# Turning probabilities, convolution and merged branch with VectorE and DRAM instead of TensorE, in a hybrid decoder layer

## The chip, the cores and the metric

The kernel runs on one core of one Trainium2 chip. The metric is the device time of one execution in microseconds (us). A core has TensorE (matrix products, PE in the profile; PEld is its weight load), VectorE (DVE), ScalarE (ACT), GpSimd (POOL) and SyncE (SP), which run side by side, each through its own queue in order, and wait for each other through semaphores.

## The reference

One sub-layer of a decoder on 256 tokens and 2048 features, in float32. Two token mixers run in parallel, each with a SiLU gate path, then a merge by sigmoid gates and an output projection:

```python
h = _rmsnorm(x, pre_norm_g)
proj = h @ w_in
(q_a, c_kv, k_rope, z_mla, c_in, b_gate, c_gate, z_conv, g_mla, g_conv) = split(proj)

q = _rmsnorm(q_a, q_a_norm_g) @ w_q_b        # 16 heads, 128 + 64 (rotary)
kv = _rmsnorm(c_kv, kv_a_norm_g) @ w_kv_b    # 16 heads, 128 + 128
attn = causal_softmax(q k^T / sqrt(192)) v   # 256 x 2048
y_mla = (attn * silu(z_mla)) @ w_o_mla

u = c_gate * c_in
conv = conv_w[0] * u[s-2] + conv_w[1] * u[s-1] + conv_w[2] * u[s]
y_conv = (b_gate * conv * silu(z_conv)) @ w_o_conv

merged = sigmoid(g_mla) * y_mla + sigmoid(g_conv) * y_conv
x = x + _rmsnorm(merged @ w_out, post_norm_g)
```

## The kernel before

Every float32 operand of a product is split into a high and a low part (`split_act`, lines 227 to 234: ScalarE writes the high part, VectorE subtracts it to get the low one), and a product is three matmuls: high x high, high x low, low x high. All matmuls are recorded at line 88, all turns on TensorE at line 91.

The weights come from DRAM in units of 1 MB (`raw`, three buffers, issued by SyncE at line 148). A unit is split in two halves `whi` and `wlo` of 128x1024 (five buffers each). `take(i)` hands out unit i and, before that, writes out the loads up to unit i+2 and the split of unit i+1. The order of units is the list `order`, which follows the order of the work.

A schedule by a timeline model orders each engine's instructions; what is wrapped in `tc.keep_in_program_order` is pinned behind everything written before it on its engine. TensorE's matmuls and turns, and the DMAs that GpSimd issues, are all pinned.

Stage 1, the head loop (16 heads, 29 to 44 us each in the chain): for head h, `z` (the gate, one unit), `scores(h)` (`sc`), and the four units of `channels(h, 0..3)` (`cv`), which compute one 512-wide column block of one of the four convolution inputs, h % 4 naming which one and h // 4 naming the block j. Beside them stand the head groups: `a` (the matmuls `qn` and `kn` of the next two heads), `r` (`qr`), and every fourth head `v` (`vv`). `scores` leaves the probabilities `p` (128 queries x 384: block one sees 128 keys, block two 256; last written at line 589). `turn(h, p)` turns its three 128x128 blocks on TensorE into a PSUM bank `tp` and splits that into `pt`; `values(h, ...)` multiplies with v (`o`) and writes `at_f`.

The convolution needs `u` shifted by one and two tokens: `taps(j, t)` (t is the half of 128 tokens) moves shifted copies `mv` and the tap weights `cw` with DMAs on GpSimd's queue (line 664) in steps that the loop calls with `next(tap)`. When the gates are there, `channels_join(j, t)` multiplies them in, in place, in `cv_f` (seen by rows of tokens as `cv_t`).

Stage 2, four column groups c, each four sweeps of four units (`tokens(c, n, cols)`, matmuls `sq`): the two gates from `x_both`, then `at_both` x w_o_mla, then `cv_both` x w_o_conv. `split_branch` splits `at_f` into `at_both` in the first sweep of group 0; `turn_branch` turns the eight convolution blocks on TensorE (bank `ct`, four turns each) in its second and third sweep. The memory of `at_both` and `cv_both` is the one that the head loop's temporaries held. The merged blocks `m` (two per group, in the tile `sg`) are turned on TensorE by `features` (bank `mt`) into `m_both`, after the next group's first sweep.

Stage 3: `out`, four column groups of four units from `m_both`; the last merged group is turned after the first unit of the first group. The end is the norm and the store.

Of the kernel before, what the change touches and what calls it, by code (L numbers as in the profile page):

```python
# [11 lines left out]
F32 = mybir.dt.float32  # L12
# [6 lines left out]
P = 128  # L19
# [63 lines left out]
def tile_layer(ctx: ExitStack, tc: tile.TileContext, xw, x, pos, pvec, post_g, wc, wz, wcv, wkr, wqk, wqr, wv, cwr, wsq, out):  # L83
# [6 lines left out]
    def transpose(*a):  # L90
        return tc.keep_in_program_order(nc.tensor.transpose(*a))  # L91
# [7 lines left out]
    top.tile([P, 184], F32, name="top_pad")  # L99
    wpool = ctx.enter_context(tc.tile_pool(name="wpool", bufs=1))  # L100
    psum = ctx.enter_context(tc.tile_pool(name="psum", bufs=1, space=PSUM))


    plan = []
# [104 lines left out]
    def bank(name, tag="mm", bufs=4):  # L209
        return psum.tile([P, 512], F32, name=name, tag=tag, bufs=bufs)  # L210
# [16 lines left out]
    def split_act(hi, lo, src, keep=False):  # L227
        a = nc.scalar.activation(hi, src, AF.Copy)  # L228
        b = nc.vector.tensor_tensor(lo, src, hi.bitcast(F32), op=ALU.subtract)  # L229
        if keep:  # L230

            tc.keep_in_program_order(a)
            tc.keep_in_program_order(b)
# [57 lines left out]
    def temp(name, shape=(P, S), dt=F32, bufs=2, tag=None):  # L291

        tag, n = tag or name.rstrip("0123456789_"), shape[-1]
        if n % LINE == 0:
            return bp.tile(list(shape), dt, name=name, tag=tag, bufs=bufs)
        return bp.tile([P, -(-n // LINE) * LINE], dt, name=name, tag=tag, bufs=bufs)[:, :n]


    def split_scaled(dst, src, k):
# [251 lines left out]
    def scores(h):  # L551

        (qn, kn), qr = groups["a", h // HG], groups["r", h // HG]
        j = h % HG
        sc = bank(f"sc{h}", tag="st", bufs=1)
        t0, t1 = slice(0, P), slice(P, S)
        mm = matmul
        o = sc[:, :S].rearrange("p (i k) -> p i k", i=2)
        mm(o, qn[0][:, j, t0], kn[:, :, j, :P], start=True, stop=False)
        mm(sc[:, :P], qn[1][:, j, t0], kn[:, 0, j, :P], start=False, stop=False)  # L560
        mm(o, qr[:, j, t0], kr[:, :, :P], start=False, stop=True)
        o = sc[:, S:]
        product(o, [a[:, j, t1] for a in qn], [kn[:, i, j, :] for i in range(2)], True, False)
        for i in range(2):
            mm(o, qr[:, j, t1], kr[:, i, :], start=False, stop=i == 1)
        if h == 0:
            temp("pad", (P, 4 * LINE), bufs=1)
        p = temp("p", (P, 3 * P), bufs=1)
        half = temp("sc_half", (P, P), bufs=1)
        nc.scalar.activation(half[:, :], sc[:, P:S], AF.Copy)  # L570
        nc.vector.tensor_tensor(p[:, :P], sc[:, :P], half[:, :], op=ALU.add)
        nc.vector.tensor_tensor(p[:, :P], p[:, :P], mask[:, :P], op=ALU.add)
        nc.vector.tensor_tensor(p[:, P:], sc[:, S:], mask[:, P:], op=ALU.add)
        mx, sm, rs = temp("mx", (P, NT)), temp("sm", (P, NT)), temp("rs", (P, NT))
        nb = temp("nb", (P, NT))
        for t in range(NT):
            o = slice(t * P, (2 * t + 1) * P)
            nc.vector.reduce_max(mx[:, t : t + 1], p[:, o], axis=mybir.AxisListType.X)
        nc.vector.tensor_scalar(nb[:, :], mx[:, :], -SCALE, None, op0=ALU.mult)
        for t in range(NT):  # L580
            o = slice(t * P, (2 * t + 1) * P)
            nc.scalar.activation(
                p[:, o], p[:, o], AF.Exp, bias=nb[:, t : t + 1], scale=SCALE,
                accum_out=sm[:, t : t + 1],
            )
        nc.vector.reciprocal(rs[:, :], sm[:, :])
        for t in range(NT):
            o = slice(t * P, (2 * t + 1) * P)
            nc.vector.tensor_scalar(p[:, o], p[:, o], rs[:, t : t + 1], None, op0=ALU.mult)
        return p  # L590

    def turn(h, p):

        tp = bank(f"tp{h}", tag="st", bufs=1)
        for b in range(3):
            transpose(tp[:, b * P : (b + 1) * P], p[:, b * P : (b + 1) * P], ident[:, :])
        pt = temp("pt", (P, 2, 3 * P), F32R, 1)
        split_act(pt[:, 0, :], pt[:, 1, :], tp[:, : 3 * P])
        return pt

    def values(h, pt, sz):
# [52 lines left out]
    def channels_join(j, t):  # L654
        u, w = cv_t[:, j, t, :], cv_w[:, t, :]
        nc.vector.tensor_tensor(u, u, w, op=ALU.mult)

    def taps(j, t):

# [35 lines left out]
    for h in range(H):  # L695

        tapped = h % 4 == 2 or (h > 0 and h % 4 == 0) or h == H - 1
        sz_new = silu("sz", project(u_head[h][0], f"z{h}"))
        if h == 0:
            latent_turn("qa", qa, "q_g", (("st", 1), ("o", 1)))  # L700

            def turn_keys():
                latent_turn("ckv", ckv, "kv_g", (("mm", 4), ("mm", 4)))
                next(table_parts)

            channels(h, 0, turn_keys)
            for i in first:
                make(*i)
            key_rope()
            channels(h, 1)  # L710
            channels(h, 2)
            p = scores(h)
        elif h == 1:

            pt = turn(0, p)
            channels(h, 0)
            values(0, pt, sz)
            p = scores(h)
            channels(h, 1)
            channels(h, 2)  # L720
            pt = turn(h, p)
        else:
            p = scores(h)
            channels(h, 0)
            channels(h, 1)
            pt = turn(h, p)
            if tapped:
                next(tap)
            channels(h, 2)
            values(h, pt, sz_new)  # L730
            if tapped:
                next(tap)
        for i in made[h]:
            make(*i)
        if h == 1:
            values(h, pt, sz_new)
        sz = sz_new
        channels(h, 3)
        if h % 4 == 0 and h > 0:
            for t in range(NT):  # L740
                channels_join(h // 4 - 1, t)
        if h % 4 == 1:
            tap = taps(h // 4, 1)
            next(tap)
        elif h % 4 == 3 and h + 1 < H or h == H - 2:
            tap = taps(h // 4, 0)
            next(tap)
    for t in range(NT):
        channels_join(3, t)


    bstack.close()
# [8 lines left out]
            hs = slice(h, h + 2)  # L761
            split_act(at_both[:, hs, :S], at_both[:, hs, S:], at_f[:, hs, :], True)

    def turn_branch(i):

        j, t = divmod(i, NT)
        turned(f"ct{i}", cv_t[:, j, t, :], cv_both, j, t)

    def turned(name, src, both, c, t):
        tp = bank(name, tag=("st", "o")[t], bufs=1)  # L770
        for j in range(4):
            transpose(tp[:, j * P : (j + 1) * P], src[:, j * P : (j + 1) * P], ident[:, :])
        ks, ts = slice(4 * c, 4 * c + 4), slice(t * P, (t + 1) * P)
        lo = slice(t * P + S, (t + 1) * P + S)
        split_act(both[:, ks, ts], both[:, ks, lo], tp[:, :].rearrange("p (k q) -> p k q", k=4))

    def tokens(c, n, cols):

        pss = [bank(f"sq{c}_{n}_{t}") for t in range(NT)]
        for kk in range(4):  # L780
            w = take(u_d[c][n][kk])
            if c == 0 and n == 0:
                split_branch(kk)
            if c == 0 and n in (1, 2):
                turn_branch(4 * (n - 1) + kk)
            for t in range(NT):
                for k4 in range(4):
                    k = 4 * kk + k4
                    a = [cols[:, k, o + t * P : o + (t + 1) * P] for o in (0, S)]
                    product(pss[t][:, :], a, w(k4, 512), k == 0, k == KD - 1)  # L790
        return pss
# [4 lines left out]
    def features(c, m, m_both):  # L796

        for t in range(NT):
            turned(f"mt{c}_{t}", m[t], m_both, c, t)

    waiting = m_both = None
    for c in range(4):
# [18 lines left out]
        for t in range(NT):  # L821
            nc.vector.tensor_tensor(m[t][:, :], pss[t][:, :], m[t][:, :], op=ALU.mult)
        pss = tokens(c, 3, cv_both)
        for t in range(NT):
            y = gates[1][t]
            nc.vector.tensor_tensor(y[:, :], pss[t][:, :], y[:, :], op=ALU.mult)
            nc.vector.tensor_tensor(m[t][:, :], m[t][:, :], y[:, :], op=ALU.add)
        waiting = m
    def out_product(ps, t, w, kk):
        ts = slice(t * P, (t + 1) * P)  # L830
# [6 lines left out]
            out_product(pss[t], t, w, kk)  # L837

    pss = [bank(f"out0_{t}") for t in range(NT)]
    out_products(pss, take(u_out[0][0]), 0)  # L840
    features(3, waiting, m_both)
    main.close()


# [35 lines left out]
    for c in range(3):  # L880
        if c:
            pss = [bank(f"out{c}_{t}") for t in range(NT)]
        for kk in range(0 if c else 1, 4):
            out_products(pss, take(u_out[c][kk]), kk)
        for t in range(NT):
            out_block(c, t, pss[t])
# [99 lines left out]
```

## Time and profile before

| | before |
|---|---|
| median of 3 runs | 1053.18 us (1053.15 to 1053.72) |
| profiled execution | 1052.91 us |
| its span, first to last instruction | 1050.9 us |
| TensorE busy | 1041.9 us, 99% |
| VectorE busy | 670.0 us, 64% |
| ScalarE busy | 560.3 us, 53% |
| GpSimd busy | 71.4 us, 7% |
| granted TensorE clock | 0.998 |

A row of the chain gives the start in us from the span's start, the length, and the piece of work with its count of instructions. A row of a timeline gives start, length, engine, line, operation, output <- input, and in brackets the idle time before it and what ended that. A group row (line, engine, operation, shapes, count) gives busy us and mean ns. TensorE's matmuls are pipelined, so the length of one is a latency, and a busy TensorE isn't one at its peak. In a table of windows each pair is the engine's busy us and its instruction count.

### The profile page before, as it was taken

Reading aid. Unit: us, or ns where it says so; the run is one execution under the profiler, and the core shown is the slowest. Engines: PE = TensorE matmul, PEld = TensorE weight load, DVE = VectorE, ACT = ScalarE, POOL = GpSimd, SP = SyncE. Lnnn points to the kernel's source line nnn. Section 1 sums busy time; section 2 is a strip of 40 time slices with the busy share of each in tenths; the row PEclk is TensorE's granted clock in tenths of the full one; section 3 lists DMA queues with packets and bytes.
Section 4 is the critical chain, followed back from the end, with each engine's and each line's share of the span. In section 5 each row is a group of like instructions: output and inputs, shape, how many; then the busy total and the mean of one; then the engine's idle time right before and its main releaser. Section 6 shows DMA issues by size and latency. Waiting matters only on the chain.

```text
span 1050.9 us, 12889 instructions
## 1 busy us (share of the span) xinstructions
PE 1041.9 (99%) x4934; PEld 874.3 (83%) x4934; DVE 670.0 (64%) x954; ACT 560.3 (53%) x770; POOL 71.4 (7%) x147
## 2 busy tenths in 40 slices
PE   9999999999999999999999999999999999999996
PEld 8888888888888888888888888888888888888885
DVE  7588668676686777866777764554554455445562
ACT  7776556556665566655655464444434434444450
POOL 7620011000110001100011000000000000000000
PEclk9999999999999999999999999999999999999999
DMA  8745566455665555845567555455555555558542
GB/s 332 298 173 200 201 219 207 165 210 200 210 215 196 189 192 175 273 172 193 188 203 236 202 184 196 166 195 200 190 187 184 200 200 190 176 195 314 196 171 80
DMA packets 33884, 212.13 MB, mean 202 GB/s; under 512 B 4320, under 2 KB 5024, under 8 KB 10912
## 3 DMA queue, kind: packets, MB, share of 16 engines
q1 hardware_dynamic: 29808, 197.54, 52.1%
q0 software_dynamic: 3584, 10.50, 4.2%
q10 hardware_dynamic: 432, 3.29, 0.8%
q8 instruction: 38, 0.62, 0.2%
q14 instruction: 22, 0.18, 0.0%
HBM read 205.05 MB, written 2.10 MB: 197 GB/s over the span
## 4 chain that ended last, share of the span: by engine, by line
PE 98%; issue 1%; DVE 0%; POOL 0%; ACT 0%; POOLq 0%; DVEq 0%; ACTq 0%
PE cv L88 33%; PE sq L88 33%; PE z L88 8%; PE out L88 7%; PE qn L88 2%; PE kn L88 2%; PE qa L88 2%; PE vv L88 2%; PE ckv L88 2%; PE sc L88 1%; PE qr L88 1%; PE o L88 1%; PE tp L91 0%; PE idle L88 0%; PE kr L88 0%
## 5 line engine op out<-in xcount | busy, mean ns | idle before, releaser
L229 DVE TENSOR_TENSOR wlo<-raw,whi 128x1024 fp32r<-128x1024 f32 (+1 forms) x370 | 440.3, 1199 | 309.4 <-ACT whi L228 285.5
L228 ACT ACTIVATE whi<-raw 128x1024 fp32r<-128x1024 f32 (+1 forms) x372 | 383.5, 1036 | 379.2 <-PE sq L88 186.3
L88 PE MATMUL cv<-whi,x_both 128*128 128x512 f32 x1024 | 325.4, 391 | 0.0
L88 PEld LDWEIGHTS cv<-whi,x_both 128*128 128x128 f32 x1024 | 192.3, 188 | 38.9
L88 PE MATMUL cv<-wlo,x_both 128*128 128x512 f32 x512 | 199.5, 390 | 0.0
L88 PE MATMUL sq<-whi,x_both 128*128 128x512 f32 x512 | 160.2, 391 | 0.0
L88 PEld LDWEIGHTS sq<-whi,x_both 128*128 128x128 f32 x512 | 96.1, 188 | 19.9
L88 PEld LDWEIGHTS cv<-wlo,x_both 128*128 128x128 f32 x512 | 96.2, 188 | 18.5
L88 PE MATMUL sq<-wlo,x_both 128*128 128x512 f32 x256 | 99.6, 389 | 0.0
L88 PE MATMUL sq<-whi,at_both 128*128 128x512 f32 x256 | 80.4, 391 | 0.0
L88 PE MATMUL sq<-whi,cv_both 128*128 128x512 f32 x256 | 79.5, 389 | 0.0
L88 PE MATMUL out<-whi,m_both 128*128 128x512 f32 x256 | 79.2, 390 | 0.0
L88 PE MATMUL z<-x_both,whi 128*128 128x512 f32 x256 | 60.7, 389 | 0.0
L88 PEld LDWEIGHTS sq<-whi,cv_both 128*128 128x128 f32 x256 | 48.0, 188 | 10.0
L88 PEld LDWEIGHTS sq<-whi,at_both 128*128 128x128 f32 x256 | 48.1, 188 | 9.9
L88 PEld LDWEIGHTS out<-whi,m_both 128*128 128x128 f32 x256 | 48.0, 188 | 9.9
L88 PEld LDWEIGHTS z<-x_both,whi 128*128 128x128 f32 x256 | 48.0, 188 | 9.9
L88 PEld LDWEIGHTS sq<-wlo,x_both 128*128 128x128 f32 x256 | 48.1, 188 | 9.8
L88 PE MATMUL sq<-wlo,at_both 128*128 128x512 f32 x128 | 49.8, 389 | 0.0
L88 PE MATMUL sq<-wlo,cv_both 128*128 128x512 f32 x128 | 49.8, 389 | 0.0
L88 PE MATMUL out<-wlo,m_both 128*128 128x512 f32 x128 | 49.8, 389 | 0.0
L88 PEld LDWEIGHTS z<-x_both,wlo 128*128 128x128 f32 x256 | 32.8, 191 | 1.2
(208 smaller groups left out, 1031.1 us busy)
## 6 DMA issues: line engine op xcount, KB each, us to landing
raw<-wsq_dram SPq DMA_DIRECT2D x80, 1024.0 KB, 4.7
raw<-wcv_dram SPq DMA_DIRECT2D x64, 1024.0 KB, 4.8
raw<-wz_dram SPq DMA_DIRECT2D x16, 1024.0 KB, 4.8
raw<-wqk_dram SPq DMA_DIRECT2D x8, 1024.0 KB, 6.0
cw<-cwr_dram POOLq DMA_DIRECT2D x24, 256.0 KB, 5.7
raw<-wc_dram SPq DMA_DIRECT2D x4, 1024.0 KB, 9.9
raw<-wv_dram SPq DMA_DIRECT2D x4, 1024.0 KB, 6.7
cv_f<-x_dram SPq DMA_DIRECT2D x1, 2048.0 KB, 9.5
```

Source lines behind the costliest of these rows:

```text
L88: return tc.keep_in_program_order(nc.tensor.matmul(*a, **kw))
L228: a = nc.scalar.activation(hi, src, AF.Copy)
L229: b = nc.vector.tensor_tensor(lo, src, hi.bitcast(F32), op=ALU.subtract)
```

## The change

The 112 turns on TensorE of `tp`, `ct` and `mt` are replaced. Each tile of 128 tokens by n x 128 columns (n = 3 for the probabilities, 4 for a convolution or merged block) goes this way: VectorE turns every 32x32 block into a second tile (`via`, one buffer; for the merged blocks the tile of the other gate); four DMAs, one for each quarter of 32 partitions, write it to a DRAM tile `far` in pieces of n x 32 numbers so that each row of `far` is one row of the turned tile; one DMA brings it back to the place it came from. All five stand on GpSimd's queue in program order, and the one back waits for the four. The split then reads the turned tile from chip memory, not from PSUM, through `by_rows` and `quarters`, which only reorder the view, and it is pinned.

The order changes too. The split of the probabilities comes later: in odd heads but the last before the group `a`, with `values` behind that group; in the others behind what `made` names, with `values` behind the fourth convolution unit. `channels_join` for t = 1 comes one head earlier, at h % 4 == 3, and turns its block at once. The last join's `via` is the tile `mv2`. The merged blocks are turned right where they are made, both with their DMAs out before the DMAs back, and the last group's split comes before the third unit of stage 3, not after its first. The sixteen turns of the two latents (`lt_qa`, `lt_ckv`) stay on TensorE.

```diff
@@ -99,6 +99,8 @@
     top.tile([P, 184], F32, name="top_pad")
     wpool = ctx.enter_context(tc.tile_pool(name="wpool", bufs=1))
     psum = ctx.enter_context(tc.tile_pool(name="psum", bufs=1, space=PSUM))
+    dram = ctx.enter_context(tc.tile_pool(name="dram", bufs=1, space=bass.MemoryType.DRAM))
     plan = []
@@ -294,6 +296,40 @@
         if n % LINE == 0:
             return bp.tile(list(shape), dt, name=name, tag=tag, bufs=bufs)
         return bp.tile([P, -(-n // LINE) * LINE], dt, name=name, tag=tag, bufs=bufs)[:, :n]
+    def turned(src, via, n):
+        via = via[:, : P * n]
+        v = via.rearrange("p (q k x) -> p q k x", q=4, k=n)
+        nc.vector.transpose(v.rearrange("p q k x -> p k q x"), src)
+        far = dram.tile([P, P * n], F32, name="far", tag=f"far{n}", bufs=2)
+        def go():
+            f = far[:, :].rearrange("(q y) (i m) -> i y q m", q=4, i=4)
+            for i in range(4):
+                m = via[32 * i : 32 * i + 32, :].rearrange("y (q m) -> y q m", q=4)
+                tc.keep_in_program_order(nc.gpsimd.dma_start(out=f[i], in_=m))
+        def come(dst):
+            tc.keep_in_program_order(nc.gpsimd.dma_start(out=dst, in_=far[:, :]))
+        return go, come
+    def turned_back(src, via, n):
+        go, come = turned(src, via, n)
+        go()
+        come(src)
+    def by_rows(t, n):
+        return t.rearrange("p (i k x) -> p k i x", i=4, k=n)
+    def quarters(t):
+        return t.rearrange("p k (i x) -> p k i x", i=4)
+    def via():
+        return temp("via", (P, 512), bufs=1)
     def split_scaled(dst, src, k):
@@ -587,15 +623,14 @@
         for t in range(NT):
             o = slice(t * P, (2 * t + 1) * P)
             nc.vector.tensor_scalar(p[:, o], p[:, o], rs[:, t : t + 1], None, op0=ALU.mult)
+        turned_back(p[:, :], via(), 3)
         return p
-    def turn(h, p):
-        tp = bank(f"tp{h}", tag="st", bufs=1)
-        for b in range(3):
-            transpose(tp[:, b * P : (b + 1) * P], p[:, b * P : (b + 1) * P], ident[:, :])
+    def turn(p):
         pt = temp("pt", (P, 2, 3 * P), F32R, 1)
-        split_act(pt[:, 0, :], pt[:, 1, :], tp[:, : 3 * P])
+        hi, lo = (pt[:, j : j + 1, :].rearrange("p o (k q) -> p (o k) q", k=3) for j in range(2))
+        split_act(quarters(hi), quarters(lo), by_rows(p[:, :], 3), True)
         return pt
     def values(h, pt, sz):
@@ -654,6 +689,7 @@
     def channels_join(j, t):
         u, w = cv_t[:, j, t, :], cv_w[:, t, :]
         nc.vector.tensor_tensor(u, u, w, op=ALU.mult)
+        turned_back(u, via() if t or j < 3 else temp("mv2", (P, 512), bufs=1, tag="mv2x"), 4)
     def taps(j, t):
@@ -695,6 +731,8 @@
     for h in range(H):
         tapped = h % 4 == 2 or (h > 0 and h % 4 == 0) or h == H - 1
+        early_values = h % 2 and h < H - 1
         sz_new = silu("sz", project(u_head[h][0], f"z{h}"))
         if h == 0:
             latent_turn("qa", qa, "q_g", (("st", 1), ("o", 1)))
@@ -712,41 +750,43 @@
             p = scores(h)
         elif h == 1:
-            pt = turn(0, p)
             channels(h, 0)
-            values(0, pt, sz)
+            values(0, turn(p), sz)
             p = scores(h)
             channels(h, 1)
             channels(h, 2)
-            pt = turn(h, p)
         else:
             p = scores(h)
             channels(h, 0)
             channels(h, 1)
-            pt = turn(h, p)
             if tapped:
                 next(tap)
             channels(h, 2)
-            values(h, pt, sz_new)
             if tapped:
                 next(tap)
         for i in made[h]:
+            if i[0] == "a":
+                pt = turn(p)
             make(*i)
-        if h == 1:
-            values(h, pt, sz_new)
+            if i[0] == "a":
+                values(h, pt, sz_new)
+        if h > 0 and not early_values:
+            pt = turn(p)
         sz = sz_new
         channels(h, 3)
+        if h > 0 and not early_values:
+            values(h, pt, sz_new)
         if h % 4 == 0 and h > 0:
-            for t in range(NT):
-                channels_join(h // 4 - 1, t)
+            channels_join(h // 4 - 1, 0)
+        if h % 4 == 3:
+            channels_join(h // 4, 1)
         if h % 4 == 1:
             tap = taps(h // 4, 1)
             next(tap)
         elif h % 4 == 3 and h + 1 < H or h == H - 2:
             tap = taps(h // 4, 0)
             next(tap)
-    for t in range(NT):
-        channels_join(3, t)
+    channels_join(3, 0)
     bstack.close()
@@ -761,18 +801,15 @@
             hs = slice(h, h + 2)
             split_act(at_both[:, hs, :S], at_both[:, hs, S:], at_f[:, hs, :], True)
-    def turn_branch(i):
-        j, t = divmod(i, NT)
-        turned(f"ct{i}", cv_t[:, j, t, :], cv_both, j, t)
-    def turned(name, src, both, c, t):
-        tp = bank(name, tag=("st", "o")[t], bufs=1)
-        for j in range(4):
-            transpose(tp[:, j * P : (j + 1) * P], src[:, j * P : (j + 1) * P], ident[:, :])
+    def split_turned(src, both, c, t):
         ks, ts = slice(4 * c, 4 * c + 4), slice(t * P, (t + 1) * P)
         lo = slice(t * P + S, (t + 1) * P + S)
-        split_act(both[:, ks, ts], both[:, ks, lo], tp[:, :].rearrange("p (k q) -> p k q", k=4))
+        split_act(quarters(both[:, ks, ts]), quarters(both[:, ks, lo]), by_rows(src, 4), True)
+    def split_channels(i):
+        j, t = divmod(i, NT)
+        split_turned(cv_t[:, j, t, :], cv_both, j, t)
     def tokens(c, n, cols):
@@ -782,7 +819,7 @@
             if c == 0 and n == 0:
                 split_branch(kk)
             if c == 0 and n in (1, 2):
-                turn_branch(4 * (n - 1) + kk)
+                split_channels(4 * (n - 1) + kk)
             for t in range(NT):
                 for k4 in range(4):
                     k = 4 * kk + k4
@@ -796,7 +833,7 @@
     def features(c, m, m_both):
         for t in range(NT):
-            turned(f"mt{c}_{t}", m[t], m_both, c, t)
+            split_turned(m[t][:, :], m_both, c, t)
     waiting = m_both = None
     for c in range(4):
@@ -821,10 +858,16 @@
         for t in range(NT):
             nc.vector.tensor_tensor(m[t][:, :], pss[t][:, :], m[t][:, :], op=ALU.mult)
         pss = tokens(c, 3, cv_both)
+        steps = []
         for t in range(NT):
             y = gates[1][t]
             nc.vector.tensor_tensor(y[:, :], pss[t][:, :], y[:, :], op=ALU.mult)
             nc.vector.tensor_tensor(m[t][:, :], m[t][:, :], y[:, :], op=ALU.add)
+            steps.append(turned(m[t][:, :], y[:, :], 4))
+        for go, _ in steps:
+            go()
+        for t, (_, come) in enumerate(steps):
+            come(m[t][:, :])
         waiting = m
     def out_product(ps, t, w, kk):
         ts = slice(t * P, (t + 1) * P)
@@ -837,8 +880,11 @@
             out_product(pss[t], t, w, kk)
     pss = [bank(f"out0_{t}") for t in range(NT)]
-    out_products(pss, take(u_out[0][0]), 0)
-    features(3, waiting, m_both)
+    for kk in range(3):
+        w = take(u_out[0][kk])
+        if kk == 2:
+            features(3, waiting, m_both)
+        out_products(pss, w, kk)
     main.close()
@@ -880,7 +926,7 @@
     for c in range(3):
         if c:
             pss = [bank(f"out{c}_{t}") for t in range(NT)]
-        for kk in range(0 if c else 1, 4):
+        for kk in range(0 if c else 3, 4):
             out_products(pss, take(u_out[c][kk]), kk)
         for t in range(NT):
             out_block(c, t, pss[t])
```

## The prediction

> **What bounds the kernel now.** I read the page first: busy shares, the granted clock, the chain that ended last.
>
> ```profile
> PE 1041.9 (99%) x4934; PEld 874.3 (83%) x4934; DVE 670.0 (64%) x954; ACT 560.3 (53%) x770; POOL 71.4 (7%) x147
> PEclk9999999999999999999999999999999999999999
> ...
> PE 98%; issue 1%; DVE 0%; POOL 0%; ACT 0%; POOLq 0%; DVEq 0%; ACTq 0%
> ```
>
> TensorE is busy all the time at full clock, and 98% of the chain is TensorE. Busy matmuls overlap, so the test is whether TensorE ever waits. The view of waits, TensorE alone, has one row, at the start:
>
> ```profile
> PE idle L88 <- POOL hpi L252: 1.1, 1, 1.1
> ```
>
> So any TensorE instruction taken out shortens the run by its slot, and any wait put in front of TensorE lengthens it by its whole length. The chain in order of time gives the slots: each row's start, its length, and the matmuls in it. Around head 0, head 1 and an even head (the seventh), and then in the last two stages:
>
> ```profile
> 90.38 1.40 PE qr L88 x8
> 91.78 5.47 PE cv L88 x24
> 97.24 5.54 PE z L88 x32
> 102.78 0.33 PE tp L91 x3
> 103.11 5.49 PE cv L88 x24
> ...
> 110.11 10.91 PE cv L88 x48
> ...
> 121.36 2.80 PE qn L88 x16
> 124.15 2.79 PE kn L88 x16
> ...
> 346.64 10.89 PE cv L88 x48
> 357.53 0.33 PE tp L91 x3
> 357.86 5.47 PE cv L88 x24
> ...
> 363.90 1.40 PE qr L88 x8
> 365.30 5.47 PE cv L88 x24
> ...
> 622.10 0.44 PE ct L91 x4
> ...
> 713.01 0.87 PE mt L91 x8
> ...
> 955.08 5.45 PE out L88 x24
> ```
>
> The pieces follow each other without gaps. The rows with L91 are the turns on TensorE. How many there are stands in the view of line 91:
>
> ```profile
> L91 PE MATMUL tp<-ident,p x48: 270/271/275, 102.6 to 588.5; 128*128 128x128 f32 x48
> L91 PE MATMUL ct<-ident,cv_f x32: 270/272/273, 621.9 to 663.7; 128*128 128x128 f32 x32
> L91 PE MATMUL mt<-ident,sg x32: 270/273/273, 712.8 to 961.1; 128*128 128x128 f32 x32
> ```
>
> **What is removed.** 48 + 32 + 32 = 112 turns. One is shown with 271 ns, but that is a latency: three take 0.33 us of the chain, four 0.44, eight 0.87, so one costs 0.11 us. The groups make 16 x 0.33 + 8 x 0.44 + 4 x 0.87 = 5.28 + 3.52 + 3.48 = 12.28 us. Here the Trainium skill differs: "TensorE: Matmul & The Clock Gate", Part 4: PE-mode transpose, gives a bf16 turn about 275 ns inside a kernel, close to the 271 shown; taken as time won that would make 30.8 us of 112. I take the chain.
>
> **What is added: the way of the probabilities.** For each head, behind the scaling of p: one VectorE block turn, four GpSimd DMAs to DRAM (one per 32 partitions), a wait for all four, one DMA back, then the split on ScalarE and VectorE, now pinned in program order. TensorE needs the result at `values`. The rows:
>
> ```profile
> 99.58 0.55 DVE L589 TENSOR_SCALAR p<-p,rs 128x128 f32<-128x128 f32 x2
> 114.38 0.55 DVE L589 TENSOR_SCALAR p<-p,rs 128x128 f32<-128x128 f32 x2
> 351.38 0.55 DVE L589 TENSOR_SCALAR p<-p,rs 128x128 f32<-128x128 f32 x2
> ```
> ```profile
> L228 ACT ACTIVATE pt<-tp x16: 468/470/480, 103.8 to 589.5; 128x384 fp32r<-128x384 f32 x16
> L229 DVE TENSOR_TENSOR pt<-tp,pt x16: 548/550/551, 105.5 to 590.8; 128x384 fp32r<-128x384 f32 x16
> ```
> ```profile
> L664 POOL DMA_DIRECT2D mv<-cv_f x24 | 12.9, 540 | 211.7 <-issue 84.7 <-DVE at_f L351 73.5 <-DVE kn L229 42.5
> ```
> ```profile
> DMA to landing us min/median/max: 1.6/2.9/5.6
> ```
> ```profile
> DMA to landing us min/median/max: 3.4/5.7/9.3
> ```
>
> The first landing row is that of the tile mv (chip memory to chip memory), the second that of cw (read from DRAM), both issued by GpSimd.
>
> - Block turn of 128x384: no row shows one. I take 0.55 us, the VectorE row with as many elements; twice that if it runs at half that rate.
> - Four DMAs out: three issues of 0.54 us go ahead of the last, 1.62 us; its landing is unseen. Ends 1.6 and 5.6 us from mv's row; I take the median 2.9, since these are smaller than most of mv's.
> - DMA back, 192 KB from DRAM: between mv's 2.9 and cw's 5.7, so 4.3 us. The floor is mv's 1.6, the ceiling cw's 9.3.
> - Split: 0.47 + 0.55 us.
>
> Sum L = 0.55 + 1.62 + 2.9 + 4.3 + 1.02 = 10.4 us; with both landings at their floor 6.4, with both at their ceiling 18.1 (18.6 with the slow block turn). Handoffs are left out.
>
> Against it stands the room that TensorE's other work leaves, from p ready to `values`, by the rows:
> - Even heads from 2: the scores end at 346.64, p is ready at 351.93, 5.3 us later. TensorE then has 10.89 + 5.47 + 1.40 + 5.47 = 23.2 us of other matmuls in the new order: room 17.9.
> - Odd heads from 3: 10.89 + 5.47 + 2.80 + 2.79 = 22.0: room 16.7. Head 15 (a cv unit of 5.47 in place of qn and kn): 16.5.
> - Head 1: p at 114.93, 4.8 after the scores; 10.91 + 2.80 + 2.79 = 16.5: room 11.7.
> - Head 0: p only at 100.13, since VectorE does other work between; `values` is due at 90.38 + 1.40 + 5.47 + 5.54 + 5.49 = 108.28: room 8.1.
>
> So 15 heads hide L, and head 0 waits 10.4 - 8.1 = 2.3 us (0 to 10). That is the one wait in my sum.
>
> **Who waits behind the new waits.** GpSimd's queue stops at the DMA back until the four have landed; behind it stand the taps' mv and cw loads and the next block's DMAs. A turned head holds GpSimd about 2.2 + 2.4 + 0.5 = 5 us of a head's 30, and the taps are used a head later: nothing. ScalarE and VectorE stop at the pinned split; behind it stand the weight splits whi and wlo, for which TensorE waits. Their lead:
>
> ```profile
> L229 DVE TENSOR_TENSOR wlo<-raw,whi 128x1024 fp32r<-128x1024 f32 (+1 forms) x370 | 440.3, 1199 | 309.4 <-ACT whi L228 285.5
> ```
> ```profile
> 356.25 1.06 ACT L228 ACTIVATE whi<-raw 128x1024 fp32r<-128x1024 f32 x1 [3.45 <-PE cv L88]
> ```
>
> By the five whi buffers this half belongs to the cv unit that starts at 365.30. It is done at 357.31, and with wlo's 1.20 at 358.5: the splits may slip by 6.8 us unseen. The pinned split stands behind unit 2's and the next unit's splits, about 11 us after the scores, and its data come at 5.3 + 9.4 = 14.7: held 4 us, inside the lead. VectorE's own load grows by 16 x 0.55 and 16 turns of 128x512, about 20 us, from
>
> ```profile
> 344.00:600.00 256.00, 256.00 (x1271) 216.95 (x1270) 184.68 (x302) 150.48 (x220) 15.39 (x29) 1.00 0.60 205
> ```
>
> where VectorE (fourth pair) has 184.68 of 256 us: no bound. If the splits fell behind all the same, TensorE would pay the excess over 6.8.
>
> **Convolution and merge.** A convolution block has until its turn in the second stage, 20 us and more: nothing. Merged blocks of the first three column groups have a whole sweep of 21.8 us (four units of 5.45): nothing. The last group is tight, hence the move behind two more output units:
>
> ```profile
> 956.71 0.69 DVE L827 TENSOR_TENSOR sg<-sg,sg 128x512 f32<-128x512 f32 x1
> ```
>
> Ready 957.4, block turn 0.69, last issue at 959.7, landed 962.6, back 966.9, split 967.9. TensorE gets there at 955.08 + 3 x 5.45 = 971.4: hidden by 3.5; nothing, up to 5 us with the longest landings.
>
> The passage between stages is the place I trust least:
>
> ```profile
> 603.89 1.15 ACT L228 ACTIVATE at_both<-at_f 128x512 fp32r<-128x512 f32 x2 [2.45 <-DVE cv_f L656]
> ```
>
> ScalarE's first write to at_both waits for memory that the last joins hold. Now the last blocks' buffers are held until their DMAs have landed, one block behind the other: 603.7 + 0.69 + 1.62 + 2.9 = 608.9, then 0.54 + 1.62 + 2.9 more: 614. If ScalarE stops there with weight splits behind it, it stops 10 us longer, and 10 - 6.8 = 3.3 us reach TensorE; if the splits stand ahead of it, nothing. I take nothing, as splits that are ready sooner may be ordered ahead.
>
> **Sum.** The profiled execution took 1052.91 us (span 1050.9, 2.0 around it), 0.27 below the median 1053.18. 1052.91 - 12.28 + 2.3 = 1042.9, as a median 1043.2. Its own range, 0 to 5 us of waiting: 1040.9 to 1045.9.
>
> **Rivals.** What a measurement can tell from no change is about 0.2%, 2.1 us.
> - *Longer landings (slower).* The way through DRAM takes longer than L and heads wait. For it: small pieces, 512 B and less, written beside weight loads that keep the DMA engines at 0.60 in the row above; cw's 9.3. Against: 10.4 is well below the 16.5 of most heads. Heads 0 and 1 pay first: L - 8.1 + L - 11.7 = 12.28 at L = 16.0; beyond that the change loses. At 18.1: 10.0 + 6.4 + 6 x 1.4 + 7 x 0.2 + 1.6 = 27.8, that is 1068.7. The Trainium skill speaks for it in "DMA: Bandwidth & Descriptors", Specifications: below 512 B a DMA does read-modify-write, and a piece of p is 384 B. No run here shows that. Chance 0.22 (slower 0.20, same 0.02).
> - *GpSimd held by VectorE.* If each of the five issues first waits out a weight split of 1.20 us, L is 16.4, heads 0 and 1 pay 8.3 + 4.7 = 13.0, and the time is 1053.9. Against: mv's 24 issues took 540 ns in the mean beside a VectorE at 72%. The Trainium skill's "SBUF — State Buffer", in its part on a bandwidth-pool intuition that's wrong, has a GpSimd DMA at about 3100 ns beside a VectorE copy for 620 alone, which in every issue would give well over 1100; the trace does not agree. Chance 0.07 (same 0.03, slower 0.04).
> - *Splits late at the stage passage.* 3.3 us, more with longer landings: 1046 to 1051. Chance 0.15, faster.
> - *Turns worth their 271 ns:* 30 us gained, 1025. The gapless chain speaks against it. Chance 0.02.
> - *Freed slots give nothing,* because VectorE or the weights pace the kernel after all: 1053. VectorE at 72% and ScalarE's 3.45 us waits for TensorE speak against. Chance 0.02 (same 0.01, slower 0.01).
>
> **Numbers.** Forecast 0.52. Faster 0.52 + 0.15 + 0.02 = 0.69; same 0.02 + 0.03 + 0.01 = 0.06; slower 0.20 + 0.04 + 0.01 = 0.25. The range goes from a shade under all hidden, 1040, through the stage passage up to 1060, two thirds of the way to the 1068.7 of the first rival; above lie about half of it and the worse part of the second, 0.15, and below 0.02.
>
> **What would show it.** Right: no tp, ct or mt rows; z and sc pieces 0.33 us nearer per head; TensorE waiting only near 108, for pt; the sq stage shorter by 0.44 eight times. Wrong: TensorE waiting at `values` in every head (landing over 12 us for both ways together), weight splits waiting for at_both at 600, or GpSimd issues well over 0.54. It is all wrong if the four DMAs out land far later than mv's 5.6.

## The result: 5.5% slower, and the profile after

| | before | after |
|---|---|---|
| median | 1053.16 us (4 runs) | 1111.37 us (4 runs, 1109.04 to 1113.6) |
| ratio to before | | 1.0552, 95% interval 1.053 to 1.0575 |
| profiled execution, its span | 1052.91, 1050.9 us | 1110.96, 1109.2 us |

The forecast was 1043.2 us, in a range of 1040 to 1060: wrong in sign and size. The page of after, in the lines that were shown of before:

```profile
PE 1044.3 (94%) x4822; PEld 873.1 (79%) x4822; DVE 689.1 (62%) x986; ACT 562.2 (51%) x770; POOL 160.3 (14%) x307
...
PEclk9999998998989989989989999999999999999998
...
PE 77%; DMA 9%; DVE 7%; issue 3%; POOL 2%; ACT 1%; POOLq 0%; DVEq 0%; ACTq 0%
```

The 112 turns are gone (4934 - 4822), yet TensorE is not busier than 94%, only 77% of the chain is TensorE (DMAs 9%, VectorE 7%), and the clock has dips in the first half. The view of waits, TensorE alone, in us in total, times, and the longest:

```profile
PE o L88 <- DVE pt L231: 50.5, 8, 9.7
PE out L88 <- ACT m_both L230: 2.1, 1, 2.1
PE idle L88 <- POOL hpi L254: 1.1, 1, 1.1
PE out L88 <- DVE m_both L231: 0.6, 1, 0.6
```

The eight waits for the split probabilities, from TensorE's timeline (the wait in brackets):

```profile
111.56 0.57 PE L88 MATMUL o<-pt,vv_hi 128*128 128x512 f32 x1 [2.98 <-DVE pt L231]
133.38 0.47 PE L88 MATMUL o<-pt,vv_hi 128*128 128x512 f32 x1 [2.02 <-DVE pt L231]
175.72 0.76 PE L88 MATMUL o<-pt,vv_hi 128*128 128x512 f32 x1 [6.41 <-DVE pt L231]
257.61 0.77 PE L88 MATMUL o<-pt,vv_hi 128*128 128x512 f32 x1 [9.50 <-DVE pt L231]
330.53 0.77 PE L88 MATMUL o<-pt,vv_hi 128*128 128x512 f32 x1 [5.93 <-DVE pt L231]
410.51 0.77 PE L88 MATMUL o<-pt,vv_hi 128*128 128x512 f32 x1 [8.11 <-DVE pt L231]
483.73 0.77 PE L88 MATMUL o<-pt,vv_hi 128*128 128x512 f32 x1 [5.92 <-DVE pt L231]
565.43 0.77 PE L88 MATMUL o<-pt,vv_hi 128*128 128x512 f32 x1 [9.67 <-DVE pt L231]
```

These are heads 0 and 1 and the even heads 2 to 12. No odd head from 3 on waits, and neither does head 14, the only even head from 2 on that has no group `r`. So it is not the length of the way through DRAM alone; something in those even heads adds to it. Head 6 on VectorE, from its timeline:

```profile
322.53 1.71 DVE L459 TENSOR_TENSOR rp_b<-f,sin_t 32x256 f32<-32x256 f32 x4
...
325.55 0.41 DVE L460 TENSOR_TENSOR f<-rp_a,rp_b 128x256 f32<-128x256 f32 x1
...
327.67 1.22 DVE L231 TENSOR_TENSOR wlo<-raw,whi 128x1024 fp32r<-128x1024 f32 x1
328.92 0.87 DVE L231 TENSOR_TENSOR qr<-f,qr 64x256 fp32r<-64x256 f32 x2
329.82 0.56 DVE L231 TENSOR_TENSOR pt<-p,pt 128x384 fp32r<-128x384 f32 x1
```

and the DMA back on GpSimd's queue:

```profile
307.63 2.22 POOL L312 DMA_DIRECT2D far<-via  x4 [8.03 <-DVE via L305]
314.72 0.56 POOL L316 DMA_DIRECT2D p<-far  x1 [4.87 <-DMA far<-via]
```

The data were back at 314.72 + 5.8 (the landing of `p` in this head, the longest of all) = 320.5. TensorE was ready for `o` at 330.53 - 5.93 = 324.6. The split came at 329.82, directly behind the split of `qr`, which ends the rotary work of group `r`: in those heads `turn` is written behind `r`, and the pin puts the split behind everything written before it on VectorE, the rotary pieces among them. These can only start when TensorE has done `qr`:

```profile
318.50 0.64 PE L88 MATMUL qr<-qa,wlo 128*128 128x256 f32 x4
```

`qr` ends at 319.1, only 5.5 us before `o` is due, since one convolution unit stands between them. From there to the split VectorE is busy without a gap, with the rotary pieces and, between them, weight splits, taps and gates.

In heads 4, 8 and 12 the wait is 2 to 4 us longer. GpSimd's queue around head 4:

```profile
222.88 2.18 POOL L312 DMA_DIRECT2D far<-via  x4 [23.44 <-DVE via L305]
230.12 0.56 POOL L316 DMA_DIRECT2D cv_f<-far  x1 [5.06 <-DMA far<-via]
...
232.70 1.09 POOL L700 DMA_DIRECT2D cw<-cwr_dram  x2
233.78 2.22 POOL L312 DMA_DIRECT2D far<-via  x4
248.84 0.56 POOL L316 DMA_DIRECT2D p<-far  x1 [12.85 <-ACT cv_f L682]
```

At the end of heads 3, 7 and 11 a convolution block goes its way (first two rows); the taps' loads, written behind it, cannot go before 230, and meet the probabilities of the next head in one burst. The bracket names ScalarE; what the queue waited for were the four landings, 13.3 us in the median there. The DMA issues of 230 to 250 (count, KB each, median us to landing), the chain, the table of windows (last three columns: granted clock, DMA share, GB/s), and a row of VectorE's timeline:

```profile
cw<-cwr_dram POOLq DMA_DIRECT2D x3, 256.0 KB, 11.8
...
far<-via POOLq DMA_DIRECT2D x4, 48.0 KB, 13.3
```

```profile
233.24 13.20 DMA cw<-cwr_dram
```
```profile
238.00:242.00 4.00, 4.00 (x19) 3.31 (x18) 0.26 (x2) 1.11 (x2) 0.00 (x0) 1.00 1.00 353
```
```profile
244.61 0.69 DVE L716 TENSOR_TENSOR mv<-mv,cw 128x512 f32<-128x512 f32 x1 [1.40 <-DMA cw<-cwr_dram]
```

The DMA engines are full. VectorE's two joins then wait 1.40 and 1.26 us for `cw`, the second until 246.56, and behind them come the rotary chain and the split. The probabilities are late too: the DMA back, issued at 248.84, took 4.8 to land, so they were there at 253.6, while TensorE had been ready at 257.61 - 9.50 = 248.1. The split came later still, at 256.90.

The third cost was not in the prediction at all. The windows after the waits of heads 0, 1 and 2:

```profile
112.00:114.00 2.00, 2.00 (x11) 2.00 (x10) 0.74 (x2) 0.38 (x1) 0.00 (x0) 0.50 0.89 377
...
133.30:135.30 2.00, 1.92 (x10) 1.71 (x11) 1.68 (x3) 1.44 (x5) 0.00 (x0) 1.00 0.41 168
...
176.00:180.00 4.00, 4.00 (x12) 3.23 (x12) 0.85 (x2) 0.38 (x1) 0.00 (x0) 0.50 0.10 41
180.00:184.00 4.00, 4.00 (x27) 3.64 (x26) 0.72 (x1) 2.12 (x2) 0.00 (x0) 0.99 0.00 0
```

After the 2.02 us wait of head 1 the clock is granted at 1.00, after the 2.98 of head 0 and the 6.41 of head 2 at 0.50. The chain shows what that costs behind head 2, and where it costs most (head 8):

```profile
175.72 1.40 PE o L88 x4
177.12 7.01 PE z L88 x32
...
410.51 1.41 PE o L88 x4
411.91 7.36 PE z L88 x32
```

At full clock `o` takes 0.57 and the z unit 5.54. Over the six long waits `o` is 5.0 us longer in all and z (6.48 to 7.36) 8.1; `o` and the scores behind head 0 add 1.4 (1.22 + 1.72 against 0.57 + 0.94). That makes 14.5 us, 2.2 for each long wait. The Trainium skill, "TensorE: Matmul & The Clock Gate", Part 1 (the clock gate), has TensorE at half clock after an idle window of about 3.4 us, and as long again until it is back. The traces agree only in part. The return, after about 3 to 5 us in this run, fits. The bound here lies between waits of 2.02 and 2.98 us, but over all runs there is no sharp one. Behind a wait of 1.88 us, in head 10 of the kernel with both faults mended (below), the clock was halved; behind one of 2.92, in head 0 of the kernel without the taps' loads, it stayed full:

```profile
446.42:448.42 2.00, 2.00 (x7) 1.58 (x6) 2.00 (x3) 0.96 (x3) 0.00 (x0) 0.56 0.04 16
```
```profile
111.40:113.40 2.00, 1.97 (x14) 1.88 (x15) 0.63 (x2) 0.52 (x2) 0.00 (x0) 1.00 0.90 381
```

Waits of 0.9 to 1.23 us behind the start left it full, and every wait of 4.06 us and more halved it; those of 1.88 to 2.98 us did either, and what decides it is open.

The span's balance: 1050.9 - 12.3 (turns) + 53.2 (waits) + 14.5 (clock) + 2.6 = 1108.9 of 1109.2. The last term lies behind the work: from the end of SyncE's last store issue to the end of the span are 3.0 us before and 5.6 after, and the profile shows nothing in them that differs.

### The profile page after: what moved, and what is told of

Its sections match the earlier page's. It is cut to its first block, busy times and chain, and to the rows that moved or that the text cites. A ratio compares the mean times of both kernels' runs of the same rounds, so it can differ in the third digit from the quotient of the medians.

```text
span 1109.2 us, 13010 instructions
## 1 busy us (share of the span) xinstructions
PE 1044.3 (94%) x4822; PEld 873.1 (79%) x4822; DVE 689.1 (62%) x986; ACT 562.2 (51%) x770; POOL 160.3 (14%) x307
## 4 chain that ended last, share of the span: by engine, by line
PE 77%; DMA 9%; DVE 7%; issue 3%; POOL 2%; ACT 1%; POOLq 0%; DVEq 0%; ACTq 0%
PE sq L88 31%; PE cv L88 21%; PE z L88 6%; PE out L88 6%; DMA cw<-cwr_dram 4%; DMA far<-via 3%; DVE wlo L231 2%; PE qa L88 2%; PE vv L88 2%; PE ckv L88 2%; PE kn L88 2%; PE qn L88 2%; PE o L88 1%; PE sc L88 1%; DMA raw<-wsq_dram 1%
## 5 line engine op out<-in xcount | busy, mean ns | idle before, releaser
L88 PE MATMUL cv<-whi,x_both 128*128 128x512 f32 x1024 | 321.3, 390 | 0.0
L312 POOL DMA_DIRECT2D far<-via x92 | 50.7, 558 | 333.4 <-DVE via L305 333.4
L88 PE MATMUL z<-x_both,whi 128*128 128x512 f32 x256 | 69.1, 428 | 0.0
L88 PEld LDWEIGHTS z<-x_both,whi 128*128 128x128 f32 x256 | 54.0, 214 | 11.8
L88 PE MATMUL o<-pt,vv_hi 128*128 128x512 f32 (+1 forms) x32 | 15.5, 483 | 50.5 <-DVE pt L231 50.5
L312 POOL DMA_DIRECT2D far<-sg x32 | 17.5, 554 | 309.5 <-DVE sg L305 242.3
L88 PEld LDWEIGHTS o<-pt,vv_hi 128*128 128x128 f32 x32 | 7.6, 239 | 53.6 <-issue 50.1
```

The source lines that it names most:

```text
L88: return tc.keep_in_program_order(nc.tensor.matmul(*a, **kw))
L312: tc.keep_in_program_order(nc.gpsimd.dma_start(out=f[i], in_=m))
```

## The experiments

Three theories of the waits in even heads stood at the start: A, the pinned split stands behind the rotary chain; B, the way through DRAM is too long; C, the taps' loads come late and hold VectorE's joins. Times without a ratio are single runs, the others medians.

**The way of the probabilities taken out.**

```diff
-        turned_back(p[:, :], via(), 3)
+        v = via()[:, : 3 * P].rearrange("p (q k x) -> p k q x", q=4, k=3)
+        nc.vector.transpose(v, p[:, :])
```

> The probabilities get their block turn but none of their five DMAs; the split reads them where they stand (the output is not the reference's). Theory A (the split is pinned behind the rotary chain of group r, so in even heads TensorE waits for that chain and not for the data): heads 2, 6 and 10 still wait about 6 us each before their values, heads 4, 8 and 12 fall from 8 to 9.7 to about 6, heads 0 and 1 stop waiting; about 1095 us. Theory B (the way through DRAM is too long): no head waits, about 1046 us. Theory C (the taps' loads come late on GpSimd's queue and VectorE's joins hold the split): waits of heads 2 to 12 fall to under 3 us, about 1060 us.

1108.41 us. Waits of TensorE:

```profile
PE o L88 <- DVE pt L231: 48.9, 6, 10.6
```

Without a single DMA for the probabilities the even heads wait as before (head 6: 6.31); only heads 0 and 1 are free. B falls for heads 2, 6 and 10. Heads 4, 8 and 12 did not get shorter (9.0 to 10.6), against the expectation: the loads of the taps are late all the same, and VectorE's joins wait 19.5 us for `cw` in this kernel (9.0 in after). For these three the run shows that the joins alone make so long a wait, not that the data were in time.

**The split ahead of group r.**

```diff
-            if i[0] == "a":
+            if i[0] == "a" or i[0] == "r" and h > 0:
                 pt = turn(p)
...
-        if h > 0 and not early_values:
+        if h > 0 and not early_values and not any(i[0] == "r" for i in made[h]):
             pt = turn(p)
```

> In even heads the pinned split is written ahead of group r, not behind it. Theory A: heads 2, 6 and 10 stop waiting (their data land 4 us before the values are due); heads 4, 8 and 12, whose data land late, keep 5 to 7 us; about 1076 us. Theory B: the waits stay, about 1111 us. Theory C: the joins still stand ahead of the split, so the waits stay within 1 us, about 1110 us.

1087.57 us, between the expectations of A and the others. Heads 2, 6, 10 and 4, 8, 12 part: 6 went to 0.97, 4 only to 7.17.

```profile
247.39 0.77 PE L88 MATMUL o<-pt,vv_hi 128*128 128x512 f32 x1 [7.17 <-DVE pt L231]
315.10 0.47 PE L88 MATMUL o<-pt,vv_hi 128*128 128x512 f32 x1 [0.97 <-DVE pt L231]
```

So the place of the split is the whole cause in one half of the even heads but for 1 us, and one of several in the other. In head 4 TensorE was ready at 240.2, the data were back at 239.38 + 3.4 = 242.8, and the split came at 246.69, directly behind the taps' last join: the late loads hold it in both ways.

**The taps without their loads.** Each DMA of `taps` becomes a fill by GpSimd (the two pieces of a shifted copy become one fill):

```diff
-            tc.keep_in_program_order(nc.gpsimd.dma_start(out=dst, in_=src))
+            tc.keep_in_program_order(nc.gpsimd.memset(dst, 0.5))
```

> The taps' DMAs (shifted copies and tap weights) are replaced by GpSimd memsets of the same tiles (the output is not the reference's). Theory A: heads 2, 6 and 10 keep their 6 us, heads 4, 8 and 12 fall to about 6, since the burst of five loads beside the trip is gone; about 1103 us. Theory B: the waits of 2 to 12 shrink by no more than 2 us each, about 1100 us. Theory C: heads 2 to 12 stop waiting, about 1055 us.

1100.51 us; heads 4, 8 and 12 wait 5.96, 7.82 and 5.62, close to the others but for head 8, and heads 2, 6 and 10 are nearly as they were (5.86 to 5.87). Taking away the loads alone leaves theory A's wait.

**Both: the split first, and the taps' loads written ahead of the block's way** (at the end of heads 3, 7, 11). This is added to the edit of the split ahead of group r:

```diff
-        if h % 4 == 3:
-            channels_join(h // 4, 1)
         if h % 4 == 1:
...
             next(tap)
+        if h % 4 == 3:
+            channels_join(h // 4, 1)
```

> The split ahead of group r, and at the end of heads 3, 7 and 11 the taps' loads are written ahead of the convolution block's trip on GpSimd's queue. If heads 4, 8 and 12 wait because those loads stand behind that trip and meet the probabilities' trip in one burst: their waits fall from 7 to 8 us to about 1, as in heads 2, 6 and 10, and the slow clock behind them goes, 1087.6 - 3 x 6.7 - 3 x 2.3 = about 1060 us. If the burst has another cause: about 1087 us. The 3 us of head 0, 2 of head 1 and the wait in stage 3 stay.

1061.89 us, ratio 1.0081 (1.0065 to 1.0096). The long waits are gone:

```profile
PE o L88 <- DVE pt L231: 11.7, 8, 2.9
```
```profile
241.40 0.47 PE L88 MATMUL o<-pt,vv_hi 128*128 128x512 f32 x1 [0.97 <-DVE pt L231]
```

Head 4: 9.50 with both faults, 7.17 with only the split moved, 5.96 with only the loads away, 0.97 with both mended. The two stand one behind the other on VectorE, so mending one gains little. The same loads are all there; only their place changed, and the longest landing of `cw` fell from 13.2 to 8.5 us. Of the last 1 us of the even heads the chain shows this much: in head 4 the split (240.70) stands directly behind the taps' last join (240.09), with rotary pieces ahead of that, while TensorE was ready at 240.43. Whether they hold it was not tested.

**The split not pinned.**

```diff
-        split_act(quarters(hi), quarters(lo), by_rows(p[:, :], 3), True)
+        split_act(quarters(hi), quarters(lo), by_rows(p[:, :], 3))
```

> The changed kernel with the split of the probabilities at the same place in the text but not pinned. If the pin behind the rotary chain of group r is what holds it: heads 2, 6 and 10 wait about 1 us, heads 4, 8 and 12 keep 7 to 8 (late data), about 1088 us. If the order is the schedule's own and not the pin's: the waits of 6 us stay, about 1111 us.

1090.93 us. Heads 2, 6 and 10 do not wait at all, so the pin in its place was what held them. Heads 4, 8 and 12 still wait 6.57 to 8.60. New are waits of 1.9 to 2.1 us in heads 3, 7 and 11. In head 3 it is not the place of the split: the chain goes through the landing of `p` (194.62 + 4.90 = 199.52), and the split follows at once. Why its way ends so late there was not followed.

**Convolution and merge by way of DRAM, the probabilities on TensorE as before.** `turn`, the head loop and the place of `values` are those of before; the rest is that of after.

> The probabilities are turned on TensorE as before, with the loop's order of before; only the convolution blocks and the merged blocks go through VectorE and DRAM. All theories: 3.5 + 3.5 us of TensorE slots fewer, 2.7 us of waiting in stage 3 as in the changed kernel, and the slower clock behind it about 1 us: 1049 to 1050 us. If the convolution blocks' trips delay the taps (theory C) waits appear in the head loop, and it is over 1055 us.

1053.38 us, ratio 1.0002 (0.9993 to 1.0012): 4 us above the expectation; the profiled execution, 1055.62 us, is the slowest of its ten. One cause is the last merged group, with the clock at 0.50 for 6 us behind its wait:

```profile
PE out L88 <- ACT m_both L230: 5.1, 1, 5.1
PE tp L91 <- DVE p L625: 1.3, 2, 0.9
```

**The same, the last merged group on TensorE as before.**

```diff
-    for kk in range(3):
...
+    out_products(pss, take(u_out[0][0]), 0)
+    features(3, waiting, m_both)
```

> As the kernel with the probabilities on TensorE, and the last merged group on TensorE too, after the first unit of stage 3, as before. If the 5.1 us wait in stage 3 is the last group's way through DRAM beside the 3 MB loads of gb and xr, it is gone: 1053.2 - 3.5 (eight convolution blocks) - 2.6 (three merged groups) + 1.3 (two small waits of heads 5 and 13 seen there) = 1048.4 us. If the wait comes from elsewhere (weights late in stage 3), it stays and the time is 1051 or more.

1050.95 us, ratio 0.9984 (0.9975 to 0.9993), 2.5 above the expectation. The chain shows the other small wait's origin, the burst again: in this kernel too the taps' loads stand behind a block's way.

```profile
354.44 13.18 DMA cw<-cwr_dram
...
367.91 0.69 DVE mv L717
...
388.08 0.30 DVE p L625
...
388.51 0.61 PE tp L91 x3
```

SyncE's last store is issued by 1041.95, 6.0 us earlier than before, but the span ends 7.6 us behind it, where before has 3.0. The profile shows no instruction in these 4.6 us. Six of the kernels here end 3.0 or 3.1 us behind the last store issue, as before does, after and three others 5.6 or 5.7; why is open.

**The last merged group by way of DRAM, with the load of x out of its way.** The 3 MB that stage 3 loads for its end (`gb` and `xr`, issued by ScalarE) start just as this group travels: 1008.4 in after, beside its DMAs from 1008.2 on. To the kernel with the probabilities on TensorE:

```diff
-    nc.scalar.dma_start(out=xr[:, :, :], in_=x)
...
         for t in range(NT):
             out_block(c, t, pss[t])
+        if c == 0:
+            tc.keep_in_program_order(nc.scalar.dma_start(out=xr[:, :, :], in_=x))
```

> This is the kernel with the probabilities turned on TensorE and the convolution and all merged groups by way of DRAM, with one edit: the 2 MB load of x for the residual is issued by ScalarE only after the first column group of stage 3, not at its start. There the last merged group's four landings took 9.1 us (median) and the way back 6.4, at a DMA share of 0.89 to 1.02, and TensorE waited 5.1 us for m_both. Theory T (the last group is late because the 2 MB lie beside it): both landings fall to about 4 us, far is issued by 957, so m_both is there at about 957 + 4 + 0.5 + 4.3 + 0.7 = 966.5 and TensorE, due at 967.0, waits 0 to 1 us; about 5 us less, 1048.5 us. Rival (the weight loads and the small pieces are enough): the wait stays near 5 us and the time near 1053.4.

1047.53 us, ratio 0.9948 (0.9931 to 0.9964): the 5.1 us wait is 1.0, with the same weight loads beside it.

```profile
PE out L88 <- ACT m_both L230: 1.0, 1, 1.0
```

The landings fell only in part (9.1 to 6.0 out, 6.4 to 5.4 back, not the 4 expected). So the 2 MB made most of this wait. That the weights and `gb` stretch the rest of the way is likely, but no run here takes them away.

**Only where there is room (the mixed kernel).** Probabilities by way of DRAM in odd heads from 3 on, with the order of after; in the other heads on TensorE with the order of before; convolution and the first three merged groups by DRAM; the taps' loads first.

```diff
+    def by_dram(h):
+        return h % 2 and h > 1
```

> Only what has room goes through VectorE and DRAM: the probabilities of the odd heads from 3, the convolution blocks, the merged groups 0 to 2; the rest is turned on TensorE at its old place; taps' loads ahead of the block's trip. If only the placement made the loss, no wait is left: 1053.2 - 7 x 0.33 - 3.5 - 2.6 = 1044.8 us, up to 1.3 more for the small waits of heads 5 and 13. If the trips cost by themselves (DMA engines, GpSimd, VectorE's load), 1049 us or more.

1043.62 us, ratio 0.9911 (0.9898 to 0.9925): faster than both kernels.

```profile
PE idle L88 <- POOL hpi L254: 1.1, 1, 1.1
PE sq L88 <- DVE wlo L231: 0.3, 1, 0.3
```

It has 112 - 27 - 8 = 77 turns fewer than before, 8.4 us at 0.11; its span is 8.7 us shorter. Where the way has its room, it costs nothing and the turns are worth what the chain said.

> The kernel with only the odd heads' probabilities by DRAM (1043.6 us), and on top of it the last merged group by DRAM again, with the load of x late. Theory T: the eight turns on TensorE (0.87 us) go and no wait comes, 1042.8 us, at most 1043.8 with a wait of 1 us. Rival: a wait of about 5 us and slow clock behind it, 1048 to 1049.

This one, with the last merged group by DRAM too and `xr` late, has no wait of TensorE over 0.4 us but the 1.1 at its start, and takes 1043.55 us, ratio 0.991 (0.9896 to 0.9925): no difference that can be told from the one before.

## Why the prediction was wrong, by its steps

- **Turns at 0.11 us: right.** The 77 of the mixed kernel bear it out; the 271 ns rival does not.
- **The terms of L: one too small, the landing out.** Block turn, issues, way back and split were right. The groups of block turns (578 to 581 ns against 0.55) and of issues (551 ns against 0.54):

```profile
L305 DVE STREAM_TRANSPOSE via<-p x16: 578/579/581, 101.0 to 643.9; 128x384 f32<-128x384 f32 x16
```
```profile
L312 POOL DMA_DIRECT2D far<-via x92: 551/551/660, 101.9 to 666.8; - x92
```

  From the last of the four issues to the DMA back were 5.4 us in head 6 (4.87 of idle behind the issue's own 0.55) against 2.9 forecast, and 13.4 in head 4; the way back took 4.3 in the median as forecast, 5.8 at most, in head 6. So L was 0.58 + 1.65 + 5.4 + 5.8 + 1.02 = 14.5 us in head 6, within its room of 17.9. In head 4 it was 0.58 + 1.65 + 13.4 + 4.8 + 1.02 = 21.5, and 2.9 more because the four issues stood behind the taps' loads: 24.4, more than the room.
- **"15 heads hide L, and head 0 waits 2.3": this step failed.** Head 0 waited 2.98 and head 1, with the next smallest room, 2.02. In heads 2, 6 and 10 it failed but not by L: the data were back in time in head 6, and the experiment without any DMA waited just as long in all three. I measured the room against the landing of the data. The split starts at the later of the landing and the end of everything written before it on its engine. I placed it behind weight splits, about 11 us after the scores; in head 6 it came 28.4 us after them (301.43 to 329.82), behind the rotary chain, which I never placed on VectorE. In heads 4, 8 and 12 the joins and L failed together, both through the taps' late loads.
- **"Who waits behind the new waits": failed in its direction.** I asked mostly what is queued behind the split; the cost lay in what the split is queued behind. "The taps are used a head later: nothing" was wrong too for heads 4, 8 and 12: a block's way moves their loads 8 us back, into a burst in which all landings stretch.
- **GpSimd held by VectorE: wrong, as given.** 551 ns in the median beside a VectorE busy 62% of the span; 660 at most.
- **Stage passage: nothing, right.** No wait of TensorE there in after, where ScalarE stood 1.45 us before `at_both`; 0.3 us in the mixed kernel.
- **Convolution and first merged groups nothing: right for stage 2.** From the first `sq` to the first `out` 348.2 us after (660.19 to 1008.39) against 354.74, 6.5 us less; 32 ct and 24 mt turns give 6.1.
- **Last merged group "hidden by 3.5": failed,** 2.7 us of wait. Its landings were priced as everywhere else, and I did not ask what starts beside them: `gb` and `xr`.
- **The clock was left out:** a long wait cost its length and 2.2 us more.
- A small misreading: in the table of windows VectorE's 184.68 us stand in the third pair, not the fourth. The number is VectorE's.

The longer-landings rival had the right sign, and in heads 4, 8 and 12 landings of 11 to 13 us did exceed the room. As a whole its mechanism was wrong: its price, 27.8 us, spreads over all heads, while odd heads from 3 on, with less room than even ones, never waited, and half of the long waits came without a late landing.

## What to carry to other kernels

Before a wait is called hidden, place the waiting instruction on its engine: it starts at the later of its data and the end of all that the pin puts ahead of it, and a split written one group later can cost more than the transfer itself. When DMAs are put on a shared queue, follow each load that now stands behind them to its new time and ask what else moves then. Move such work only where the room is there: 77 of the 112 turns, moved, gave 0.9%, and all 112 cost 5.5%.

## What the runs showed of the hardware

After the waits of 3.0 to 9.7 us in after TensorE's clock was granted at 0.50, for about 3 to 5 us. Over all runs it was halved after every wait of 4.06 us and more and, behind the start, after none of 0.9 to 1.23; waits of 1.88 to 2.98 went either way. In a burst beside weight loads, at a DMA share of 0.87 to 1.00, four DMAs of 48 KB took 13.3 us to land where the median of their size is 4.6, and a `cw` load 13.2 where the median is 6.5. A span can end 3.0, 5.6 or 7.6 us behind its last store issue, without an instruction that shows why.
